# The heads' decay exponents taken in an earlier stage and kept in DRAM, in a one-core hybrid transformer block

## The chip, the cores and the metric

One Trainium2 chip, of which the kernel uses one core. The metric is device time in microseconds (us) of one execution. The kernel before takes 2649.45 us (median of three runs, 2648.09 to 2649.64).

## The reference

One layer of a block over 1024 latent tokens and a context of 256, all of width 1024, in float32. After a first feed-forward part, one input projection gives q, k, v, gates, and five more branches (o, u, vs, ga, gb). Two token mixers run on them and are merged:

```python
dm = b[..., :, None] - b[..., None, :] + lic[..., None, :]
dm = jnp.where(tri, dm, -jnp.inf)
m_t = jnp.maximum(a, jnp.max(dm, axis=-1))
s_ts = jnp.einsum('bhtk,bhsk->bhts', qc, kc) * jnp.exp(dm - m_t[..., None])
...
y_b = spatial_gating(jax.nn.gelu(u), jax.nn.gelu(vs), g_sgu, w_s, b_s)
mixed = jax.nn.sigmoid(ga) * (y_a @ w_a) + jax.nn.sigmoid(gb) * (y_b @ w_b)
return mixed @ w_o
```

The first is an mLSTM with 4 heads of 256, in both directions, scanned in 8 chunks of 128 tokens. Per head, direction and chunk it needs `exp(dm - m_t)`, a 128x128 block that is masked to a triangle; the code calls this P. The second, spatial gating, mixes tokens inside chunks of 128 and multiplies by gelu(u). A second feed-forward part and a norm follow.

## The kernel before

Float32 products run on TensorE as three products of rounded halves: a tile is split by an ACT cast (L145) into its high part and by a DVE subtraction (L146) into the low part. The projections use a seven-product scheme, in which one product is twelve 128x512 matmuls (`pq`, L1377). The weights pass through a queue of steps, `st`: `st.run(n)` runs n of them, and `st.part(n, 3, beside)` or `st.run(n, hook)` calls a function behind each product, so that other work is recorded beside it. Where a step's results leave PSUM, ACT copies them (L1383, L1388, L1391) or DVE adds them to such a copy (L1435), and ACT applies the gate's function (L1434, L1436).

Every engine works in order. All DMAs are issued by SP, in one order, over eight completion semaphores in rotation. A list scheduler places the recorded instructions on their engines; `tc.issue_after(x)` keeps what is recorded under it behind x. PSUM has 4 banks "mm" and 4 banks "sm".

The stages around the change, with their places in the profiled execution:

- 1173 to 1409 us, the sigmoid branches (o, ga, gb): 84 products, with `beside` behind each. It steps two generators, `background2` (further conditioning vectors) and `contexts` (the context's states). `srow`, the rows of decays from which P is built, lie in DRAM before this stage.
- 1418 to 1485 us: the vs branch, written to `vnsp` in DRAM.
- to 1580 us: the u branch. `emit_u` makes gelu(u), and for each pair of column tiles loads the mixing operand `vnp` (L1805, 512 KB) into a ring of buffers. `mix_u` (L1813 to L1819) runs the token mixing `pm` on TensorE, two DVE operations on the result and the store to `ybsp`. Behind the last ten products, `ahead(i)` is called: it starts head 0 (its P, its inter-chunk rows `ib`, its k and q) and loads the mixed rows back from `ybsp` (`yraw`, L1892), split into `yp`.
- 1580 to 1840 us: the w_b product, `pt` (L1856, weights `rawt` L1865), woven with the four heads. Scores `sp` (L1975) are k times q for eight chunks in two halves; `ptk` (L1988) transposes k; both take "sm" banks. DVE multiplies P by `sp` (L1965, `weigh`). The loop takes each chunk in both directions: `pn` (L2009, L2011), a denominator `dn` (ACT L2013, DVE L2014 and L2015), `hm` (L2018), and the state update: ACT makes `wvh` (L1691), TensorE `pu` (L1697), DVE the new `C` (L1698).

Before the change, P of a head is made inside this last stage. `rows` loads `srow`, broadcast to 128 partitions, 128x1024 for each direction (L1937). `coeff` subtracts the column's term with eight ACT operations of 128x128 (L1945) and then takes the minimum with zero and adds the mask with one DVE operation of 128x1024 (L1947). `expo` is one ACT exponential of 128x1024 (L1950). For head 0 that is in `ahead`; for heads 1 to 3 it is in the hook of the loop of the head ahead, at steps 1 to 7. Where the ACT function set changes, an ACT_TABLE_LOAD stands on ACT.

The generator's two masks (`masks[d]`, in the tile `cst`) and the column terms `COL` are loaded or made before the sigmoid stage.

## Time and profile before

| | before |
|---|---|
| median of three runs | 2649.45 us |
| runs | 2648.09, 2649.45, 2649.64 us |
| profiled execution, its own time | 2649.41 us |
| its span, first to last instruction | 2647.6 us |
| granted TensorE clock, mean | 0.998 |
| TensorE (PE) busy | 2632.7 us, 99% |
| VectorE (DVE) busy | 1947.2 us, 74% |
| ScalarE (ACT) busy | 1202.8 us, 45% |

Times inside the kernel are counted from the span's start. "PEld" is the load of weights into TensorE, which overlaps its matmuls. A row of waits gives the engine and line that waited, what it waited for, and us in total, times, longest. In a timeline row, the bracket at the end is the engine's idle time ahead of it and what ended it. "SPq" rows are DMAs being issued, not moved; the time from issue to landing is given apart.

### The profile page before, as it was taken

The numbers are of one execution on the slowest core, as the hardware profiler recorded it, in microseconds if no ns is written. First come the engines' busy times: TensorE is split into PE (matmuls) and PEld (weight loads), VectorE is DVE, ScalarE is ACT, GpSimd is POOL, SyncE is SP. The second block draws the span as 40 slices with busy tenths as digits, with TensorE's granted clock in tenths as the row PEclk, the third lists the DMA queues.
The fourth block names the chain that finished last, engine by engine and source line by source line (L and its number), as shares of the span: only waits on it lengthen the run. The fifth ranks groups of instructions, "written<-read, shape, count | busy, mean of one in ns | idle before, by whom it ended". The sixth has DMA issues, their size and how long they took to land.

```text
span 2647.6 us, 35932 instructions
## 1 busy us (share of the span) xinstructions
PE 2632.7 (99%) x12904; PEld 2213.3 (84%) x12904; DVE 1947.2 (74%) x3490; ACT 1202.8 (45%) x2167; POOL 74.2 (3%) x158
## 2 busy tenths in 40 slices
PE   9999999999999999999999999999999999999998
PEld 6998888888889878888888888888888888888887
DVE  7988688687989646787664878777568766665855
ACT  5664444444347525564443454333256444344433
POOL 0000000000000000000000002221000000000000
PEclk9999999999999999999999999999999999999999
DMA  9833344368587122356552466547341333337654
GB/s 314 308 111 136 119 163 167 112 233 309 172 278 263 65 80 91 104 184 197 188 178 105 151 218 243 175 154 267 131 142 41 127 140 115 120 123 277 200 160 178
DMA packets 201234, 452.73 MB, mean 171 GB/s; under 512 B 20320, under 2 KB 54624, under 8 KB 201056
## 3 DMA queue, kind: packets, MB, share of 16 engines
q1 hardware_dynamic: 200624, 450.05, 49.9%
q8 instruction: 101, 1.65, 0.3%
q14 instruction: 77, 0.63, 0.1%
q10 hardware_dynamic: 432, 0.39, 0.0%
HBM read 329.11 MB, written 121.32 MB: 170 GB/s over the span
## 4 chain that ended last, share of the span: by engine, by line
PE 94%; issue 2%; DMA 2%; DVE 1%; ACT 1%; POOL 0%; SPq 0%; POOLq 0%; DVEq 0%; ACTq 0%
PE qa L411 18%; PE pq L1377 17%; PE po L535 14%; PE qb L411 14%; PE pt L1856 10%; PE pr L1296 5%; PE pa L182 2%; PE pc L1165 2%; PE pb L182 2%; PE pn L2011 2%; PE pu L1697 1%; PE pn L2009 1%; PE pkc L1356 1%; PE pvc L1453 1%; PE sp L1975 1%
## 5 line engine op out<-in xcount | busy, mean ns | idle before, releaser
L146 DVE TENSOR_TENSOR ring<-rawq,ring 128x512 fp32r<-128x512 f32 x408 | 281.0, 690 | 225.5 <-ACT ring L145 224.2
L535 PE MATMUL po<-gring,wring 128*128 128x512 f32 (+1 forms) x1896 | 423.5, 384 | 0.0
L535 PEld LDWEIGHTS po<-gring,wring 128*128 128x128 f32 x1896 | 349.6, 188 | 69.9
L145 ACT CAST ring<-rawq 128x512 fp32r<-128x512 f32 x408 | 253.4, 622 | 312.3 <-PE pq L1377 87.0
L411 PE MATMUL qa<-fc,ring 128*128 128x512 f32 x1056 | 252.4, 389 | 0.0
L411 PEld LDWEIGHTS qa<-fc,ring 128*128 128x128 f32 x1056 | 198.2, 188 | 41.5 <-DVE fc L146 0.4
L1377 PE MATMUL pq<-fc,ring 128*128 128x512 f32 x864 | 208.5, 394 | 0.0
L145 ACT CAST wring<-rw 128x512 fp32r<-128x512 f32 x154 | 95.8, 623 | 217.2 <-PE po L535 183.0
L1377 PEld LDWEIGHTS pq<-fc,ring 128*128 128x128 f32 x864 | 162.2, 189 | 33.4
L1856 PE MATMUL pt<-yp,ring 128*128 128x512 f32 x768 | 184.8, 394 | 0.0
L1856 PEld LDWEIGHTS pt<-yp,ring 128*128 128x128 f32 x768 | 143.1, 188 | 28.2
L146 DVE TENSOR_TENSOR wring<-rw,wring 128x512 fp32r<-128x512 f32 x154 | 105.6, 686 | 81.4 <-ACT wring L145 81.0
L1377 PE MATMUL pq<-fa,ring 128*128 128x512 f32 x576 | 142.4, 395 | 0.0
L1377 PE MATMUL pq<-fb,ring 128*128 128x512 f32 x576 | 138.5, 394 | 0.0
L1377 PEld LDWEIGHTS pq<-fb,ring 128*128 128x128 f32 x576 | 107.7, 188 | 23.8 <-issue 0.2
L411 PE MATMUL qa<-fa,ring 128*128 128x512 f32 x528 | 127.0, 390 | 0.0
L411 PE MATMUL qa<-fb,ring 128*128 128x512 f32 x528 | 126.5, 390 | 0.0
L411 PE MATMUL qb<-fb,ring 128*128 128x512 f32 x528 | 126.5, 389 | 0.0
L411 PE MATMUL qb<-fc,ring 128*128 128x512 f32 x528 | 126.3, 389 | 0.0
L411 PE MATMUL qb<-fa,ring 128*128 128x512 f32 x528 | 126.2, 389 | 0.0
L1377 PEld LDWEIGHTS pq<-fa,ring 128*128 128x128 f32 x576 | 106.9, 188 | 22.3 <-DVE ring L146 0.2
L793 DVE SCALAR_TENSOR_TENSOR adacc<-adapg,sc,adacc 128x512 f32<-128x512 f32 x154 | 111.7, 745 | 15.7 <-DMA adapg<-in_w_ada_dram 14.7
(366 smaller groups left out, 4643.6 us busy)
## 6 DMA issues: line engine op xcount, KB each, us to landing
adapg<-in_w_ada_dram SPq DMA_DIRECT2D x144, 256.0 KB, 3.6
fsp<-fhl SPq DMA_DIRECT2D x66, 512.0 KB, 2.7
gring<-fsp SPq DMA_DIRECT2D x66, 512.0 KB, 4.1
raw<-in_w1i_dram SPq DMA_DIRECT2D x44, 512.0 KB, 5.3
graw<-fsp SPq DMA_DIRECT2D x88, 256.0 KB, 3.6
rawq<-in_w1i_dram SPq DMA_DIRECT2D x38, 512.0 KB, 3.7
rawq<-in_w2i_dram SPq DMA_DIRECT2D x38, 512.0 KB, 3.6
fsp<-p SPq DMA_DIRECT2D x66, 256.0 KB, 2.2
```

What stands on the lines that cost most here:

```text
L145: hi = S.copy(hl[:, 0, :], src)
L146: return hi, V.tensor_sub(hl[:, 1, :], src, hl[:, 0, :].bitcast(F32))
L182: T.matmul(pt, x, y, start=first and i == 0, stop=i == n - 1, skip_group_check=True)
L411: T.matmul(pt, hl[:, x, sl], pages[p][k][:, y, :], start=first and i == 0, stop=i == 11, skip_group_check=not first)
L535: T.matmul(pt[:, cs], w[:, x, sl], g[:, y, cs], start=grp and kp == 0 and i == 0, stop=kp == NFP - 1 and i == 2, skip_group_check=not grp)
L793: eng.scalar_tensor_tensor(acc, pgt, sc2[:, q, k:k + 1], acc, ALU.mult, ALU.add)
L1165: T.matmul(pt, hl[d // 4][:, x, sl], g[:, y, :], start=f == 0 and d % 2 == 0 and i == 0, stop=f == NF - 1 and i == 2, skip_group_check=True)
L1296: T.matmul(self.pt[m], pg[:, x, sl], hl[:, y, :], start=first and k == 0 and i == 0, stop=k == 3 and i == 2, skip_group_check=not first)
L1356: T.matmul(self.cp[:, o:o + 256], hl[:, x, k * 128:(k + 1) * 128], hnc[kc][:, y, :], start=p == 1 and k == 0 and i == 0, stop=p in (2, 4) ...
L1377: T.matmul(pt, hl[:, x, k * 128:(k + 1) * 128], pg[k][:, y, :], start=first and k == 0 and i == 0, stop=k == 3 and i == 2, skip_group_chec ...
L1856: T.matmul(pt, hl[:, x, k * 128:(k + 1) * 128], pg[:, y, :], start=kh + k + i == 0, stop=kh == 1 and k == 3 and i == 2)
L2011: T.matmul(pn[:, 0:257], qi[:, c_, :], self.C[d][:, c_, :], start=False, stop=c_ == 1)
```

## The change

A DRAM tensor `xsp` of 4 MB is added. A third generator, `exponents`, is stepped behind each product of the sigmoid stage. For each head, direction and half it loads 128x512 of `srow` by broadcast, waits three calls, does four ACT operations and one DVE operation on it (what `coeff` did), and two calls later has stored the result to `xsp`. There are 16 such pieces of five calls: 80 of the 84. `Head.rows` now loads P from `xsp` and `coeff` is gone; what is left in the heads' stage is the exponential, recorded at steps 4 and 6. Head 0's exponentials go by halves of 128x512, both directions' first half ahead of the second.

In `ahead`, the loads of head 0's P and most of the `yraw` loads come later: the latter behind the last `vnp` load, P behind the first w_b load. The buffers of two of the `yraw` pairs become tiles of 128x512.

```diff
+    xsp = dr.tile([2, NH, 128, 1024], F32, name="xsp")
...
+    def exponents():
+        for h_ in range(NH):
+            for d in range(2):
+                cb = COL[:, 0, 64 * d:64 * d + 40].rearrange("p (i h) -> p h i", h=4)[:, h_, 2:10]
+                for hf in range(2):
+                    x = fl("xp", "xp", (128, 512), F32, 2)
+                    nc.sync.dma_start(x, srow[d, h_, 0, 4 * hf:4 * hf + 4].rearrange("n t -> (n t)").partition_broadcast(128))
+                    x3 = x.rearrange("p (n t) -> p n t", n=4)
+                    for _ in range(3):
+                        yield
+                    for n in range(4):
+                        S.activation(x3[:, n, :], x3[:, n, :], AF.Identity, bias=cb[:, 4 * hf + n:4 * hf + n + 1], scale=-1.0)
+                    V.scalar_tensor_tensor(x3, x3, 0.0, masks[d].unsqueeze(1).to_broadcast([128, 4, 128]), ALU.min, ALU.add)
+                    yield
+                    nc.sync.dma_start(xsp[d, h_, :, hf * 512:(hf + 1) * 512], x)
+                    yield
...
+        next(bg4, None)
         steps_[0] += 1
...
-            nc.sync.dma_start(vnp[ct], vnsp.rearrange("n p c -> p n c")[:, :, ct * 128:(ct + 1) * 128])
+            ureads["v"] = nc.sync.dma_start(vnp[ct], vnsp.rearrange("n p c -> p n c")[:, :, ct * 128:(ct + 1) * 128])
...
-                nc.sync.dma_start(t, a[name][dt][:, kh * 512:(kh + 1) * 512])
+                asked_b.append(nc.sync.dma_start(t, a[name][dt][:, kh * 512:(kh + 1) * 512]))
...
-                nc.sync.dma_start(pg, srow[d, self.h, 0].rearrange("n t -> (n t)").partition_broadcast(128))
+                nc.sync.dma_start(pg, xsp[d, self.h])
...
-        def coeff(self, d, ns=range(8)):
...
-        def expo(self, d):
-            S.activation(self.pg[d], self.pg[d], AF.Exp)
+        def expo(self, d, sl=slice(0, 1024)):
+            S.activation(self.pg[d][:, sl], self.pg[d][:, sl], AF.Exp)
...
         if i == 0:
-            heads[0].rows()
             heads[0].inter()
-            early.extend(page_raws(ybsp, 0, 0, "yraw", 1))
-            early.extend(page_raws(ybsp, 0, 2, "ring2", 2))
-            early.extend(page_raws(ybsp, 1, 0, "ring2", 2))
-        elif i in (2, 3):
-            heads[0].coeff(i - 2)
+            early.extend(page_raws(ybsp, 0, 0, "yraw"))
+        elif i == 3:
             page_splits(yb, [early.pop(0) for _ in range(2)])
-        elif i == 4:
-            early.extend(page_raws(ybsp, 1, 2, "yraw", 1))
+        elif i == 5:
+            heads[0].kq()
+        elif i == 7:
+            with tc.issue_after(ureads["v"].ins):
+                early.extend(page_raws(ybsp, 0, 2, "ring2"))
+                early.extend(page_raws(ybsp, 1, 0, "ring2"))
+                early.extend(page_raws(ybsp, 1, 2, "yraw"))
             page_splits(yb, [early.pop(0) for _ in range(2)])
-        elif i == 6:
-            heads[0].kq()
-            page_splits(yb, [early.pop(0) for _ in range(2)])
+        elif i == 8:
+            with tc.issue_after(asked_b[0].ins):
+                heads[0].rows()
+            page_splits(yb, [early.pop(0) for _ in range(4)])
...
-        for d in range(2):
-            heads[0].expo(d)
+        for hf in range(2):
+            for d in range(2):
+                heads[0].expo(d, slice(hf * 512, (hf + 1) * 512))
...
-                elif t in (2, 3, 5, 6):
-                    heads[-1].coeff(int(t > 3), range(4) if t in (2, 5) else range(4, 8))
-                elif t in (4, 7):
+                elif t in (4, 6):
                     heads[-1].expo(int(t > 4))
```

Line numbers of the changed kernel differ by 1 up to the added generator, and by 20 or less behind it.

On SP, around the last load of `vnp` at the end of the u branch, before:

```order
L1922 DMA qT<-qsp 128x1024
L1805 DMA vnp<-vnsp 128x8x128
L1922 DMA qT<-qsp 128x1024
L1892 DMA yraw<-ybsp 128x512 x2
L1819 DMA ybsp<-mx 128x512 x2
L1892 DMA yraw<-ybsp 128x512
L1937 DMA P<-srow 128x1024 x2
L1892 DMA yraw<-ybsp 128x512 x3
L1805 DMA vnp<-vnsp 128x8x128
L1819 DMA ybsp<-mx 128x512
L1865 DMA rawt<-in_w_b_dram 128x512
L1892 DMA yraw<-ybsp 128x512 x3
```

The same place on SP after the change (L1944 is the load of qT, L1825 that of vnp, L1839 the store to ybsp, L1914 the yraw load, L1959 the load of P, L1885 the w_b weights):

```order
L1944 DMA qT<-qsp 128x1024
L1825 DMA vnp<-vnsp 128x8x128
L1944 DMA qT<-qsp 128x1024
L1839 DMA ybsp<-mx 128x512
L1825 DMA vnp<-vnsp 128x8x128
L1839 DMA ybsp<-mx 128x512
L1914 DMA yraw<-ybsp 128x512 x6
L1885 DMA rawt<-in_w_b_dram 128x512
L1959 DMA P<-xsp 128x1024
L1839 DMA ybsp<-mx 128x512
L1959 DMA P<-xsp 128x1024
L1885 DMA rawt<-in_w_b_dram 128x512
```

The last vnp load moved ahead of a store, of six yraw loads and of both loads of P.

On PE, from the last products of the u branch into the first heads' work, before:

```order
L1377 MATMUL pq<-fa,ring 128x512 x6
L1377 MATMUL pq<-fc,ring 128x512 x16
L1813 MATMUL pm<-wsr,vnp 128x128 x4
L1377 MATMUL pq<-fc,ring 128x512 x2
L1813 MATMUL pm<-wsr,vnp 128x128 x4
L1377 MATMUL pq<-fc,ring 128x512 x6
L1813 MATMUL pm<-wsr,vnp 128x128 x4
L1975 MATMUL sp<-qT,kT 128x128 x16
L1988 MATMUL ptk<-cst,kT 128x128 x8
L1856 MATMUL pt<-yp,ring 128x512 x12
L1988 MATMUL ptk<-cst,kT 128x128 x4
```

The same place on PE after the change (L1378 is the product, L1833 the mixing, L1989 the scores, L2002 the transposes, L1876 the w_b product):

```order
L1378 MATMUL pq<-fa,ring 128x512 x6
L1378 MATMUL pq<-fc,ring 128x512 x6
L1833 MATMUL pm<-wsr,vnp 128x128 x4
L1378 MATMUL pq<-fc,ring 128x512 x12
L1833 MATMUL pm<-wsr,vnp 128x128 x4
L1378 MATMUL pq<-fc,ring 128x512 x6
L1833 MATMUL pm<-wsr,vnp 128x128 x4
L1989 MATMUL sp<-qT,kT 128x128 x16
L2002 MATMUL ptk<-cst,kT 128x128 x8
L1876 MATMUL pt<-yp,ring 128x512 x5
L2002 MATMUL ptk<-cst,kT 128x128 x4
```

The first mixing matmuls of this piece moved ten products' matmuls earlier, and the third transpose group has five w_b matmuls ahead of it in place of twelve.

On ACT, around head 0's exponentials, before (the casts are L145, the transposes' copies kh L1990):

```order
L145 CAST yp<-yraw 128x512
L1436 ACTIVATE ug<-ug 128x512
L1950 ACT_TABLE_LOAD
L1950 ACTIVATE P<-P 128x1024 x2
L1990 CAST kh<-ptk 128x512 x2
L145 CAST ring<-rawt 128x512
```

The same place on ACT after the change (the gelu is L1437, the casts L146, kh L2004):

```order
L146 CAST yp<-yraw 128x512 x2
L1437 ACTIVATE ug<-ug 128x512
L146 CAST yp<-yraw 128x512
L1964 ACT_TABLE_LOAD
L1964 ACTIVATE P<-P 128x512
L146 CAST yp<-yraw 128x512
L1964 ACTIVATE P<-P 128x512 x3
L2004 CAST kh<-ptk 128x512 x3
```

A cast of yp now stands between the last gelu and the table load, and another between the first and the second half of the exponentials.

More of the change, by code (lines that the diff above doesn't have):

```diff
@@ L1769, in beside @@
             next(bg3, None)
+        next(bg4, None)
         steps_[0] += 1
     st.part(ns, 3, beside)
-    for g_ in (bg2, bg3):
+    for g_ in (bg2, bg3, bg4):
         for _ in g_:
@@ L1886, in _build, with page_raws @@
     tiles("w_b", AHEAD, yb, fin_b, True)
-    def page_raws(src, tb, k, tag, bufs):
-        pg = fl(tag, "yraw", (128, 1024), F32, bufs)
+    def page_raws(src, tb, k, tag):
+        if tag == "ring2":
+            pg = fl(tag, "yraw", (128, 1024), F32, 2)
         res = []
         for i in range(2):
-            r_ = pg[:, i * 512:(i + 1) * 512]
+            r_ = pg[:, i * 512:(i + 1) * 512] if tag == "ring2" else fl(tag, "yraw", (128, 512), F32, 2)
             nc.sync.dma_start(r_, src[tb, k + i])
@@ L1936, in rows @@
                 pg = self.pg[d] = fxpage("P", F32, (128, 1024))
-                nc.sync.dma_start(pg, srow[d, self.h, 0].rearrange("n t -> (n t)").partition_broadcast(128))
+                nc.sync.dma_start(pg, xsp[d, self.h])
                 for hf in range(2):
                     self.P[d, hf] = pg[:, hf * 512:(hf + 1) * 512]
-        def coeff(self, d, ns=range(8)):
-            cb = COL[:, 0, 64 * d:64 * d + 40].rearrange("p (i h) -> p h i", h=4)[:, self.h, 2:10]
-            p3 = self.pg[d].rearrange("p (n t) -> p n t", n=8)
-            for n in ns:
-                S.activation(p3[:, n, :], p3[:, n, :], AF.Identity, bias=cb[:, n:n + 1], scale=-1.0)
-            if 7 in ns:
-                V.scalar_tensor_tensor(p3, p3, 0.0, masks[d].unsqueeze(1).to_broadcast([128, 8, 128]), ALU.min, ALU.add)
-        def expo(self, d):
-            S.activation(self.pg[d], self.pg[d], AF.Exp)
+        def expo(self, d, sl=slice(0, 1024)):
+            S.activation(self.pg[d][:, sl], self.pg[d][:, sl], AF.Exp)
         def inter(self):
@@ L2077, in _build @@
     for tb in range(2):
-        early.extend(page_raws(ybsp, tb, 4, "ring2", 2))
+        early.extend(page_raws(ybsp, tb, 4, "ring2"))
     with tc.issue_after(ureads[True].ins), tc.issue_after(ureads["m"].ins):
```

2 lines of the change are left out of this document (added).

## The prediction, on record before the changed kernel ran

> **What bounds the kernel now.** I read the head of the page first: whose time is the span.
>
> ```profile
> span 2647.6 us, 35932 instructions
> PE 2632.7 (99%) x12904; PEld 2213.3 (84%) x12904; DVE 1947.2 (74%) x3490; ACT 1202.8 (45%) x2167; POOL 74.2 (3%) x158
> ```
>
> PE is busy for all but 14.9 us, and the diff takes no matmul away. So the change can win only idle time of PE, or time in which PE runs at a lower clock. PE's waits, longest first, say where that is:
>
> ```profile
> PE pm L1813 <- DMA vnp<-vnsp: 2.8, 1, 2.8
> PE pu L1697 <- DVE C L1698: 2.2, 2, 1.2
> ```
>
> One wait of 2.8 us is for the last load of the mixing operand `vnp`; two, 2.2 us together, are for the state update `C` in the heads' loops. The windows of the first (behind the length, PE's busy time; the granted clock is third from the end) show that it costs more than its idle time:
>
> ```profile
> 1570.40:1573.20 2.80, 0.05 (x1) 0.00 (x0) 1.69 (x3) 2.80 (x9) 0.00 (x0) 1.00 1.01 359
> 1573.20:1576.00 2.80, 2.74 (x17) 2.68 (x18) 2.80 (x6) 2.41 (x6) 0.00 (x0) 0.77 0.48 143
> 1576.00:1579.00 3.00, 3.00 (x13) 2.52 (x13) 1.80 (x4) 1.22 (x3) 0.10 (x1) 0.65 0.71 250
> ```
>
> PE stands still, and then runs at 0.77 and 0.65 of the clock. The chain of waits prices this (start, us, what):
>
> ```profile
> 1554.11 2.75 PE pq L1377 x12
> ...
> 1564.09 9.04 DMA vnp<-vnsp
> ...
> 1573.26 1.13 PE pm L1813 x8
> 1574.39 0.50 PE pq L1377 x2
> 1574.89 1.71 PE pm L1813 x8
> 1576.60 2.14 PE pq L1377 x6
> 1578.74 0.89 PE pm L1813 x8
> 1579.63 3.57 PE sp L1975 x32
> 1583.20 0.87 PE ptk L1988 x8
> ```
>
> ```profile
> 1573.26 1.13 PE L1813 MATMUL pm<-wsr,vnp 128*128 128x128 f32 x8 [2.82 <-DMA vnp<-vnsp]
> ```
>
> The second fence is the timeline's row, with the gap ahead of it. From 1573.26 to 1578.74 the same rows take 5.48 us; at the clock of the other rows (pm x8 0.89; 12 pq 2.75, so 0.229 each) they are 0.89 + 0.46 + 0.89 + 1.37 = 3.61. So 1.87 us are lost to the clock, and the place costs 2.82 + 1.87 = **4.69 us**.
>
> A rule of the Trainium skill bears on this: page "TensorE: Matmul & The Clock Gate", Part 1: The HAM clock gate, halves the clock after an idle window of about 3.4 us. The trace has the lower clock after 2.82 us already; by the rule the 1.87 would not have been lost here, and the place would hold 2.82.
>
> **The last `vnp` load: the 4.69 goes.** Here are SP's issues, and PE's product, around it:
>
> ```profile
> 1557.77 1.90 SPq L1819 DMA_DIRECT2D ybsp<-mx  x2
> ...
> 1564.09 0.73 SPq L1805 DMA_DIRECT2D vnp<-vnsp  x1
> ...
> 1566.66 3.79 PE L1377 MATMUL pq<-fc,ring 128*128 128x512 f32 x16
> ```
>
> SP issues in order. Before, four `yraw` loads and both P loads stand between the two (the rows left out, and the order above). After, it stands directly behind the first of those `ybsp` stores, and its buffer is free when the pm group ending about 1557.7 has run. So it is issued near 1557.8, 6.3 us earlier. Its landing times:
>
> ```profile
> DMA to landing us min/median/max: 3.8/5.3/9.0
> ```
>
> It lands between 1561.6 and 1566.8. The scheduler also puts its pm ten matmuls earlier, behind 6 of the 16 `fc` matmuls, at 1566.66 + 6 x 0.229 = 1568.0. The longest landing still leaves 1.2 us, so this wait ends: -4.69.
>
> **What is late next: the third `ptk`.** Without the gap, PE reaches its pm chain at 1570.44 and `sp` at 1570.44 + 3.61 + 0.89 = 1574.94. `sp` takes 3.57 and two ptk groups 0.87: 1579.38. Before, twelve `pt` matmuls follow; in the new order only five (5 x 0.229 = 1.15 us), so the third ptk is due at 1580.53. It needs a PSUM bank: here that is the first `sp`'s, free once DVE has multiplied both of head 0's P by it, which needs head 0's exponentials. The rows of before for that chain:
>
> ```profile
> 1580.03 0.62 ACT L145 CAST yp<-yraw 128x512 fp32r<-128x512 f32 x1
> 1580.55 0.62 ACT L1436 ACTIVATE ug<-ug 128x512 f32<-128x512 f32 x1
> 1581.19 1.28 ACT L1950 ACT_TABLE_LOAD   x1
> 1582.49 2.01 ACT L1950 ACTIVATE P<-P 128x1024 f32<-128x1024 f32 x2
> 1584.68 0.68 DVE L1965 TENSOR_TENSOR P<-P,sp 128x512 f32<-128x512 f32 x1
> ```
>
> The `yraw` loads now go out together behind vnp, from about 1559.8; by their median of 5.2 us (row below) the first data is there near 1565. From there DVE has 16 operations of about 0.7 us in a row (6 yp, 5 of the mixing, 3 more mixing or `ug`, 2 ring), 11.2 us; the last `ug` sum ends about 1576.5. ACT follows: gelu 0.63, yp 0.62, table 1.28, half a P 0.55 (half of the 1.06 of a whole one, further down, and a little), yp 0.62, the second half 0.55, DVE's product 0.68: 1581.4. The yp between these waits for `yraw` loads too:
>
> ```profile
> DMA to landing us min/median/max: 3.2/5.2/8.2
> ```
>
> One of them is issued behind a store at about 1573.4. At 5.2 it lands at 1578.6, and yp to product (0.62 + 1.28 + 0.55 + 0.62 + 0.55 + 0.68) end at 1582.9. If DVE is not late, the ug sum ends 0.7 behind its product (1574.7) and there is no wait; at the longest landing it would be 5.4. I take 1582.4, between 1581.4 and 1582.9 and nearer to the yraw case: a new wait of **+1.9** (0 to 3.0 kept). So 4.69 becomes 2.8.
>
> The Trainium skill, page "ScalarE: Activation LUTs", section What ACT_TABLE_LOAD costs, adds a drain of about 1.38 us to a load of 1.283. In the trace the load takes 1.28 and the exponential starts 0.02 after it; by the page the ptk would be 1.38 later and the sum 2647.2.
>
> **The heads' loops.** Both waits of 2.2 come through P:
>
> ```profile
> 1667.33 0.69 ACT L1945 ACTIVATE P<-P,colpg 128x128 f32<-128x128 f32 x2 [2.27 <-DMA P<-srow]
> 1667.94 0.15 ACT L2013 ACTIVATE dn<-pn 128x1 f32<-128x1 f32 x1
> ```
>
> ```profile
> 1738.15 1.21 DVE L1947 SCALAR_TENSOR_TENSOR P<-P,cst 128x1024 f32<-128x1024 f32 x1
> 1739.39 1.06 ACT L1950 ACTIVATE P<-P 128x1024 f32<-128x1024 f32 x1 [1.01 <-DVE P L1947]
> 1739.41 0.47 DVE L1698 SCALAR_TENSOR_TENSOR C<-C,colpg,pu 128x257 f32<-128x257 f32 x1
> 1739.93 0.39 PE L1697 MATMUL pu<-wvh,kh 128*128 128x258 f32 x1 [1.18 <-DVE C L1698]
> ```
>
> Head 3's loop (1738): DVE's 1.21 us for P stands ahead of C; it is removed, and 1.21 exceeds the wait: **-1.18**. Head 2's loop (1667): the coefficients wait for P's load and `dn` stands behind them; the wait on C is the other 0.99 (2.2 less 1.18). The load stays, and I let it land when it does now; then one exponential of 1.06 stands ahead of dn in place of two coefficients (0.69): **+0.4**. Whether a contiguous load of this size lands sooner, these rows bound (issue to landing in that stretch, kT being contiguous):
>
> ```profile
> kT<-ksp SPq DMA_DIRECT2D x2, 512.0 KB, 5.6
> P<-srow SPq DMA_DIRECT2D x2, 512.0 KB, 6.1
> ```
>
> Half a us is less than the exponential holds up, so I keep +0.4; if it lands a us sooner the wait goes (-1.0), and if it lands behind other loads the wait may triple (+2.0). The other 64 coefficients and 8 minima lie beside a busy PE: 0.
>
> **The sigmoid branches' stage: 0 taken.** It gains per piece (16) one load and one store of 256 KB, four ACT operations and one DVE operation of half this size:
>
> ```profile
> L1945 ACT ACTIVATE P<-P,colpg x64: 386/390/411, 1567.2 to 1737.5; 128x128 f32<-128x128 f32 x64
> ```
>
> That is 64 x 0.390 = 25.0 us on ACT and about 16 x 0.61 = 9.8 on DVE, over 250 us. The stage's fullest window for ACT (PE busy, then PEld, DVE and ACT), and the load most like the new one:
>
> ```profile
> 1160.00:1180.00 20.00, 20.00 (x92) 16.55 (x91) 17.75 (x26) 16.08 (x32) 0.00 (x0) 1.00 0.63 212
> ib<-srow SPq DMA_DIRECT2D x16, 256.0 KB, 5.3
> ```
>
> PE has no gap; per 20 us ACT gets 2.0 more and DVE 0.8, and both fit even here. A piece is used three products after its load, 3 x 2.75 = 8.2 us; the same kind of load, ib from the same rows, lands in 5.3. What hides it is that time plus the split's lead of a product; without that cover each piece could cost what a late P cost head 2, 0.99, so 0 to 15.8.
>
> **The sum.** -4.69 + 1.9 - 1.18 + 0.4 + 0 = -3.6, from the profiled execution's 2649.41 (1.8 above its span; the median of the runs shown is 2649.45): **2645.8 us**.
>
> **The rivals.**
> *No new wait, 24%.* DVE keeps pace, the third ptk finds its bank, and head 2's load lands in time: -4.69 - 1.18 - 1.0 = -6.9, **2642.5**. For it: DVE's 0.75 and 0.68 us operations have gaps in the old trace. Against it: five pt instead of twelve.
> *The new wait stands and the clock drops again, 15%.* +1.87 on the forecast: **2647.7**. For it: 0.77 and 0.65 after 2.82; against, head 3's window, whose 1.18 leaves the clock at 1.00:
>
> ```profile
> 1738.00:1744.00 6.00, 4.82 (x27) 4.02 (x26) 5.41 (x17) 3.53 (x8) 2.13 (x4) 1.00 0.13 44
> ```
>
>  By the 3.4 us of the Trainium skill's page on the clock gate, a gap of 1.9 would not lower it; the trace's 2.82 shows that less than 3.4 can, so the rival keeps its chance.
> *It doesn't do what it says, 14%.* vnp lands later than the 10.2 us it now has, because six yraw loads and P crowd it, or a few pieces of the stage show: only head 3's gain and a share of the 4.69 stay. **2648 to 2652**, 2648.2 where nothing but 1.18 is won.
> *Slower, 10%.* In the sigmoid stage the broadcast loads come late, ACT waits at the head of its queue for xp, the gelu and sum that free PSUM banks and the next weights' casts queue behind it, and PE stops. Price 0.99 each; it decides where landings pass 8.2 us (`yraw`, as large and not a broadcast, reached that). Half the pieces: 2645.8 + 7.9 = 2653.7; three quarters **2657.6**; all 2661.6.
>
> **How the numbers follow.** The forecast has 37%; with the four above that is all. About 0.2% (5.3 us) is what a measurement of this kernel can tell from no change, so faster means under 2644.1: the first rival, 24%. Slower means over 2654.8: the last, 10%. The rest, 66%, is the same. The range leaves out the last rival and the far ends of the first and fourth: 2642.3, just under the full removal, to 2651.0, in the fourth.
>
> **What would show it.** Right: no pm wait on vnp and clock 1.00 over 1570 to 1580; a wait of the third ptk near 1580.5 of 1 to 3 us behind weigh; no DVE operation on P ahead of C in head 3; sixteen ACT groups on xp with PE at 20.00 of 20. Wrong: PE rows waiting for ACT or DVE between 1170 and 1410, an ACT wait for xp, a ptk without wait, or a clock under 0.9 behind it.

## The result, and the profile after

The changed kernel takes 2662.10 us (median of six runs), the kernel before beside it 2648.14: a ratio of 1.0053, 95% interval 1.0040 to 1.0066. The forecast was 2645.8 in a range up to 2651.0. The profiled execution took 2661.46 us, 12.05 more than the one of before. The head of its page, and PE's longest waits (total, times, longest):

```profile
span 2659.6 us, 36014 instructions
PE 2637.4 (99%) x12904; PEld 2213.3 (83%) x12904; DVE 1947.8 (73%) x3498; ACT 1202.1 (45%) x2169; POOL 73.0 (3%) x158
```

```profile
PE pq L1378 <- DVE sg L1436: 5.1, 4, 2.3
PE ptk L2002 <- DVE P L1979: 2.3, 1, 2.3
PE pu L1737 <- DVE C L1741: 2.3, 1, 2.3
PE pu L1698 <- DVE C L1699: 1.5, 2, 1.0
...
PE pu L1737 <- ACT ktc L1728: 0.9, 1, 0.9
```

The wait for vnp is gone, and the third ptk waits 2.3 us, as forecast. New are the first, third and last rows: they lie in the sigmoid branches' stage (`sg` is its branches' tile, L1737 the context's state product). The busy time of the engines in 1170 to 1300 us, before and after:

```profile
1170.00:1300.00 130.00, 130.00 (x576) 106.76 (x575) 94.63 (x155) 62.80 (x129) 0.00 (x0) 1.00 0.65 209
```

```profile
1170.00:1300.00 130.00, 121.66 (x516) 97.64 (x515) 94.13 (x157) 74.28 (x182) 0.00 (x0) 0.97 0.78 252
```

PE stands still for 8.3 us, and the clock falls to 0.97 in the mean. To place the whole difference I compare when the same matmul starts in both traces, at five points: the first context state product (1172.58 us before), the last matmul group of the vs branch (1474.39), the first `sp` (1579.46), the first `pn` (1595.75), the last `pn` (1827.38). The delay against before grows or shrinks between them (the last column goes to the end of the span, which is 11.96 longer):

| us | ahead of the stage | sigmoid stage to vs branch | u branch (vnp) | third ptk | heads' loops | behind |
|---|---|---|---|---|---|---|
| forecast | 0 | 0 | -4.69 | +1.9 | -0.8 | 0 |
| measured | +1.70 | **+13.79** | -4.66 | +2.50 | -1.15 | -0.22 |

The 1.70 ahead of the stage come before anything that the change touches (1.1 of it within the first 10 us). The other runs below have 0.1 to 1.6 there, so it is part of what one execution scatters. From here on "the stage's cost" is the third column, worked out in the same way for every run from its one profiled execution. The executions of one kernel scatter: from the fastest to the slowest, 2.6 us in the changed kernel and 7.3 in the widest run below. Two rows that differ by 2 or 3 us are therefore not told apart.

### The profile page after: what moved, and what is told of

It is laid out like the page before. It is cut to its first block, busy times and chain, and to the rows that moved or that the text cites. A ratio compares the mean times of both kernels' runs of the same rounds, so it can differ in the third digit from the quotient of the medians.

```text
span 2659.6 us, 36014 instructions
## 1 busy us (share of the span) xinstructions
PE 2637.4 (99%) x12904; PEld 2213.3 (83%) x12904; DVE 1947.8 (73%) x3498; ACT 1202.1 (45%) x2169; POOL 73.0 (3%) x158
## 3 DMA queue, kind: packets, MB, share of 16 engines
q8 instruction: 101, 1.65, 0.3%
## 4 chain that ended last, share of the span: by engine, by line
PE 88%; DMA 5%; DVE 3%; issue 2%; ACT 1%; SPq 0%; POOL 0%; POOLq 0%; DVEq 0%; ACTq 0%
PE qa L412 18%; PE po L536 13%; PE qb L412 13%; PE pq L1378 13%; PE pt L1876 10%; PE pr L1297 5%; PE pa L183 2%; PE pc L1166 2%; PE pb L183 2%; DMA adapg<-in_w_ada_dram 2%; PE pn L2025 2%; PE pu L1698 1%; PE pn L2023 1%; PE pkc L1357 1%; PE pvc L1454 1%
## 5 line engine op out<-in xcount | busy, mean ns | idle before, releaser
L146 ACT CAST ring<-rawq 128x512 fp32r<-128x512 f32 x408 | 253.3, 621 | 300.4 <-PE qb L412 72.2
L1378 PE MATMUL pq<-fc,ring 128*128 128x512 f32 x864 | 211.3, 397 | 5.1 <-DVE sg L1436 5.1
L1378 PEld LDWEIGHTS pq<-fc,ring 128*128 128x128 f32 x864 | 163.4, 191 | 40.9 <-DVE sg L1436 6.8
L146 ACT CAST wring<-rw 128x512 fp32r<-128x512 f32 x154 | 95.5, 622 | 218.8 <-PE po L536 187.3
L1876 PE MATMUL pt<-yp,ring 128*128 128x512 f32 x768 | 184.9, 394 | 0.0
L1876 PEld LDWEIGHTS pt<-yp,ring 128*128 128x128 f32 x768 | 142.9, 188 | 28.4 <-DVE yp L147 0.2
L1378 PE MATMUL pq<-fa,ring 128*128 128x512 f32 x576 | 142.6, 395 | 0.1
L1378 PE MATMUL pq<-fb,ring 128*128 128x512 f32 x576 | 138.5, 394 | 0.0
L1378 PEld LDWEIGHTS pq<-fb,ring 128*128 128x128 f32 x576 | 107.6, 188 | 23.9 <-issue 0.2
L1378 PEld LDWEIGHTS pq<-fa,ring 128*128 128x128 f32 x576 | 106.8, 188 | 22.7 <-DVE ring L147 0.5
```

The lines of the kernel that those rows point to most:

```text
L146: hi = S.copy(hl[:, 0, :], src)
L1378: T.matmul(pt, hl[:, x, k * 128:(k + 1) * 128], pg[k][:, y, :], start=first and k == 0 and i == 0, stop=k == 3 and i == 2, skip_group_chec ...
L1876: T.matmul(pt, hl[:, x, k * 128:(k + 1) * 128], pg[:, y, :], start=kh + k + i == 0, stop=kh == 1 and k == 3 and i == 2)
```

## The experiments

Each kernel ran beside the kernel before on the same chip. The costs of the parts, from the traces, stand ahead, since all runs are read by them. "ACT for xp" is ACT's longest single wait, in the stage, for a piece's load or for its buffer, counted also where the trace names no end of it ("issue").

| run | median (before beside it) | stage | u branch | third ptk | heads | ACT for xp |
|---|---|---|---|---|---|---|
| the change | 2662.10 (2648.14) | 13.8 | -4.66 | 2.5 | -1.2 | 5.1 |
| no pieces | 2647.43 (2649.07) | 0.5 | -4.65 | 1.7 | -0.3 | none |
| operations only | 2649.09 (2649.16) | 2.3 | -4.63 | 1.7 | -1.6 | 0.4 |
| no load | 2650.87 (2649.07) | 5.0 | -4.63 | 1.3 | -0.1 | 2.7 |
| moves only | 2659.92 (2649.07) | 12.3 | -4.63 | 3.8 | -1.9 | none |
| loads only | 2652.85 (2649.16) | 6.1 | -4.65 | 1.7 | -2.5 | none |
| POOL's queue | 2678.53 (2648.27) | 33.1 | -4.64 | 3.7 | -2.7 | 6.7 |
| unlinked sums | 2662.50 (2648.27) | 15.9 | -4.63 | 1.5 | -2.0 | 5.7 |
| plain rows | 2658.87 (2648.27) | 12.4 | -4.65 | 1.6 | +0.3 | 4.3 |
| unread load | 2659.86 (2649.16) | 10.9 | -4.67 | 1.3 | -1.7 | 3.5 |
| small moves | 2650.45 (2648.90) | 3.0 | -4.63 | 1.9 | -1.0 | 2.0 |
| paced | 2649.12 (2649.07) | 2.6 | -4.64 | 1.2 | -1.6 | none |
| paced, more traffic | 2649.56 (2648.90) | 3.8 | -4.63 | 2.2 | -2.5 | 1.8 |
| spread, late load | 2663.85 (2649.81) | 18.2 | -4.64 | 1.7 | -2.8 | 5.7 |
| order only | 2650.10 (2649.16) | 0.6 | -4.64 | 2.0 | +3.6 | none |
| paced, exponentials first | 2648.53 (2648.27) | 1.3 | -4.65 | 2.0 | -0.4 | none |
| paced, ptk split | 2648.11 (2648.90) | 2.8 | -4.67 | -0.1 | +0.2 | none |

**Which part of a piece costs?** My theory: ACT comes to a piece's operations before its load has landed, and what frees PSUM stands behind them. Rivals: the added operations crowd out others, or the added bytes make other transfers late.

No pieces:

```diff
-        next(bg4, None)
...
-                nc.sync.dma_start(pg, xsp[d, self.h])
+                nc.sync.dma_start(pg, srow[d, self.h, 0].rearrange("n t -> (n t)").partition_broadcast(128))
```

> The changed kernel without its sixteen pieces: the sigmoid branches' stage is as before, P is loaded from the rows by broadcast, and the subtraction, minimum and mask are left out (the exponentials run on scaled raw rows, so P is not the reference's). All theories: the stage's 13.6 us of loss are gone, the 4.7 of the vnp wait stay won, the third ptk still waits about 2.4. 2645 us, 3 below the kernel before. If it stays above 2650, the loss comes from the reordered loads and not from the pieces.

2647.43 us, ratio 0.9995 (0.9986 to 1.0004). The stage is whole (0.5), so the 13.8 are the pieces'. The other terms stay, and add up to -3.3 in its trace; the medians show half of that, within what they can tell.

No load:

```diff
-                    nc.sync.dma_start(x, srow[d, h_, 0, ...].partition_broadcast(128))
...
-                        S.activation(x3[:, n, :], x3[:, n, :], AF.Identity, ...)
+                        S.activation(x3[:, n, :], ident, AF.Identity, ...)
```

> The pieces without their loads: the ACT operations read a resident tile in place of the loaded row, so P is not the reference's; operations, stores and everything else stay. If ACT's wait at the head of its queue for the xp load is the cause, the sigmoid stage loses under 2 us and the time is 2646 to 2648. If the added ACT and DVE operations crowd out what frees PSUM, the stage still loses 10 or more: 2656 to 2661. If DMA traffic is the cause, half of it is left: about 2652.

2650.87, ratio 1.0010 (1.0001 to 1.0018); the stage costs 5.0. Between the first theory's and the traffic's figure. ACT still waits here, up to 2.7 us, for the store that frees a buffer.

Moves only:

```diff
-                    for n in range(4):
-                        S.activation(x3[:, n, :], x3[:, n, :], AF.Identity, ...)
-                    V.scalar_tensor_tensor(x3, x3, 0.0, masks[d]..., ALU.min, ALU.add)
```

> The pieces' loads and stores alone, without their four ACT and one DVE operation (subtraction, minimum and mask left out, exponentials on scaled raw rows). Waiting ACT and crowding both say that the stage is whole again: 2645 to 2647. If the traffic delays the weights and the conditioning rows, the loss stays: 2656 or more.

2659.92, ratio 1.0038 (1.0025 to 1.0051): against my theory. Without any operation of ACT the stage loses 12.3. DVE's waits in its trace show another queue held up, by the conditioning rows `adapg`, which land late:

```profile
DVE adacc L794 <- DMA adapg<-in_w_ada_dram: 26.8, 19, 6.2
```

In the changed kernel that wait is 13.0 in total and at most 1.9, so the two kernels need not lose their time in the same way.

Paced:

```diff
+            sigs[:] = [plus(t, x, pt, AF.Sigmoid)]
...
+                    with tc.issue_after(sigs[0].ins) if sigs else ExitStack():
+                        nc.sync.dma_start(x, srow[d, h_, 0, ...].partition_broadcast(128))
...
+                    with tc.issue_after(sigs[0].ins):
                         for n in range(4):
                             S.activation(x3[:, n, :], x3[:, n, :], AF.Identity, ...)
```

> The whole change, but each piece's load and each piece's ACT and DVE operations are held behind the latest sigmoid recorded at their call, which spreads the sixteen pieces over the stage's 231 us in place of 126, and puts the operations products behind the load. Waiting ACT says that the loss of 13.6 falls under 2 us: 2645 to 2648, below the kernel before. Crowding says that half of it stays, since the work is the same at half the density: about 2652. Traffic says the same as crowding.

2649.12, ratio 1.0002 (0.9993 to 1.0011); the stage costs 2.6. The hold acts on the engine of the instruction named, so only ACT's operations are held; the loads are spread because two buffers are all there is. ACT no longer waits for xp. I took it that the bytes were spread too and that both stories were still open. The window that I showed for the changed kernel says more (DMA share and GB/s at the end of the row):

```profile
1170.00:1300.00 130.00, 129.22 (x569) 105.13 (x568) 99.14 (x163) 71.81 (x164) 0.00 (x0) 1.00 0.79 249
```

The paced kernel moves 249 GB/s there, the changed kernel 252, and PE stands 0.8 us in place of 8.3. What differs is where the operations and the loads stand, not how much is moved.

**Which link leads to PE?**

POOL's queue:

```diff
-                    nc.sync.dma_start(x, srow[d, h_, 0, ...].partition_broadcast(128))
+                    nc.gpsimd.dma_start(x, srow[d, h_, 0, ...].partition_broadcast(128))
...
-                    nc.sync.dma_start(xsp[d, h_, :, hf * 512:(hf + 1) * 512], x)
+                    nc.gpsimd.dma_start(xsp[d, h_, :, hf * 512:(hf + 1) * 512], x)
```

> The changed kernel with the pieces' loads and stores issued by POOL, which has nothing else to do in this stage; the same bytes, the same operations. If the pieces' DMAs, waiting at the head of SP's queue for a landing or an operation, hold up the conditioning rows and weights behind them, the stage's loss falls from 13.8 to under 5: 2650 to 2653. If the bytes themselves slow the other transfers, it stays: 2660 to 2662. If ACT's waits for xp count for themselves, something between is left.

2678.53, ratio 1.0109 (1.0094 to 1.0125). With a queue of their own the stage costs 33.1. On POOL each load stands behind a store that waits for DVE, comes later still, and ACT's longest wait for it is 6.7; the loads also land later there, at a median of 4.7 us against 4.2. The run took one wait away and made another longer, so it does not say what SP's queue costs.

Unlinked sums, for the stage's four vectors:

```diff
-                    ada_acc(V, accs[0], pgt, conds[0], k, k == 0)
+                    ada_acc(V, accs[0]..., ident.unsqueeze(1).to_broadcast([128, 4, 128]), conds[0], k, k == 0)
```

> The changed kernel, in which DVE's sums of the conditioning rows of this stage read a resident tile in place of the rows loaded (the loads are still made), so that DVE never waits for them; the last four modulation vectors are wrong by that. If late conditioning rows at the head of DVE's queue are the link from the pieces' transfers to TensorE, the stage's loss falls from 13.8 to under 5: 2650 to 2653. If the link is ACT's waits for xp or late weights, it stays above 10: 2658 to 2662.

2662.50, ratio 1.0054 (1.0041 to 1.0068); the stage costs 15.9. The waits for conditioning rows are gone (1.6 us are left) and nothing is won, so they are not the link of the changed kernel. ACT's longest wait for a piece is 5.7 here.

Plain rows:

```diff
-                    nc.sync.dma_start(x, srow[d, h_, 0, ...].partition_broadcast(128))
+                    nc.sync.dma_start(x, hsp[hf, 2 * h_ + d])
```

> The changed kernel with each piece's load taken from 128 different rows of another tensor of the same size in DRAM, in place of one row of 2 KB read for all 128 partitions; P is not the reference's. If the loads cost because of their bytes or their place in SP's queue, nothing changes: 2660 to 2662. If reading one row 128 times is slow, or slows others, the loss falls by several us: 2650 to 2656.

2658.87, ratio 1.0036 (1.0022 to 1.0050); the stage costs 12.4. The broadcast is not the main cause; the other 1.4 are within the scatter.

Unread load:

```diff
+                    y = fl("xq", "xq", (128, 448), F32, 1)
+                    nc.sync.dma_start(y, srow[d, h_, 0, ...][0:448].partition_broadcast(128))
...
+                        S.activation(x3[:, n, :], ident, AF.Identity, ...)
```

> The changed kernel, with each piece's load (448 of its 512 columns) landing in a buffer that nothing reads, and ACT's four operations reading a resident tile; operations, stores and nearly all bytes stay, and P is not the reference's. What is taken away is ACT's wait for the load. If that wait, at the head of ACT's queue, is the cause, the sigmoid stage costs what the run without loads cost, about 5: 2650 to 2652. If the loads' bytes or their places in SP's queue are the cause, it still costs 10 or more: 2656 to 2661.

2659.86, ratio 1.0035 (1.0022 to 1.0048); the stage costs 10.9. By its text that speaks for the bytes, but the edit did not do what I said. ACT waits nearly as long in all as in the change, now for the store that frees the buffer, though never longer than 3.5. The execution profiled is the fastest of its five, 4.2 under the median, so the 10.9 is rather too low:

```profile
ACT xp L1774 <- DMA xsp<-xp: 23.8, 11, 3.5
```

So it told nothing apart. Loads only, which is moves only less its stores:

```diff
-                    nc.sync.dma_start(xsp[d, h_, :, hf * 512:(hf + 1) * 512], x)
```

> The pieces' loads alone: no operations, no stores (P from the rows by broadcast, exponentials of scaled raw rows, so P is not the reference's). The loads and stores alone cost the stage 12.3. If that was because a store stands on SP right behind the load that it waits for, and holds SP's queue for it, the loss goes: under 2, about 2647. If the loads' bytes delay the other transfers, at least half stays: 2652 or more.

2652.85, ratio 1.0013 (1.0004 to 1.0022); the stage costs 6.1. About half of the 12.3 of loads and stores goes with the stores; DVE's longest wait for adapg is 5.7. By its text, that is the bytes' side, at its edge.

Operations only, which is the no-load kernel less its stores:

```diff
-                    nc.sync.dma_start(xsp[d, h_, :, hf * 512:(hf + 1) * 512], x)
```

> The pieces' ACT and DVE operations alone, on a resident tile; no loads, no stores (P from the rows by broadcast, without subtraction, minimum and mask). The run without loads cost the stage 5.0. If the added operations crowd those that free PSUM, it still costs 4 to 5: 2649 to 2651. If the stores cost it, the stage is whole: 2645 to 2647.

2649.09, ratio 1.0001 (0.9992 to 1.0011); the stage costs 2.3. This is the price of the work itself.

Order only (the kernel before, with head 0's P and six yraw loads recorded behind the last vnp load):

```diff
+        elif i == 7:
+            with tc.issue_after(ureads["v"].ins):
+                heads[0].rows()
+                early.extend(page_raws(ybsp, 0, 2, "ring2", 2))
...
+            heads[0].coeff(0)
```

> The kernel before with one part alone: head 0's P and six yraw loads behind the last vnp load; the exponents are made in the heads' stage as before. The sigmoid stage costs nothing, the 4.7 of the vnp wait is won, and the third ptk waits longer, since sixteen coefficients (6.2 us of ACT) now stand among the yp casts: 1 to 4. 2646 to 2649. If the vnp wait needed the pieces in DRAM to go, the wait is still there.

2650.10, ratio 1.0004 (0.9995 to 1.0013). The 4.64 are won without any piece in DRAM, and given back in the heads' loops (+3.6), where a wait for C grows to 2.4 and the granted clock is 0.67 behind it, over 1739 to 1744.

**Waits without bytes, bytes without waits.** Small moves:

```diff
-                    nc.sync.dma_start(x, srow[d, h_, 0, ...].partition_broadcast(128))
+                    nc.sync.dma_start(x[:, 0:16], srow[d, h_, 0, 4 * hf]...[0, 0:16].partition_broadcast(128))
...
+                    S.activation(x3[:, 0, 0:16], x3[:, 0, 0:16], AF.Identity, bias=cb[:, 4 * hf:4 * hf + 1], scale=-1.0)
...
-                    nc.sync.dma_start(xsp[d, h_, :, hf * 512:(hf + 1) * 512], x)
+                    nc.sync.dma_start(xsp[d, h_, :, hf * 512:hf * 512 + 16], x[:, 0:16])
```

> The changed kernel with loads and stores of 16 columns in place of 512: one more, short ACT operation reads the 16 loaded columns, so ACT and SP wait for the same chain of landings, and the four operations read a resident tile (P from the rows by broadcast, exponentials scaled; P is not the reference's). Bytes fall from 8.4 MB to 0.3. If the bytes cause the loss, the stage costs what the operations alone cost, about 2: 2647 to 2650. If ACT's waits cause it, most of the 13.8 stays, less what a small landing is shorter: 2653 or more.

2650.45, ratio 1.0007 (0.9998 to 1.0016); the stage costs 3.0. That is the traffic's figure, but ACT's waits had shrunk too, since the small landings are short:

```profile
ACT xp L1772 <- DMA xp<-srow: 7.2, 8, 1.9
ACT xp L1774 <- DMA xsp<-xp: 4.8, 6, 2.0
```

Paced, more traffic (on SP, behind each third product's latest sigmoid store, sixteen in the first half):

```diff
+            with tc.issue_after(puts[0].ins):
+                nc.sync.dma_start(xsq[steps_[0] // 3], hsp[0, steps_[0] % 8])
```

> The paced kernel, in which ACT has no long wait, plus sixteen copies of 256 KB from DRAM to DRAM on SP among the first half of the stage's products: with half the pieces that is at least the changed kernel's traffic there, and the result is the reference's. If the bytes cause the loss, the stage costs 8 to 14 in place of the paced 2.6: 2655 to 2661. If ACT's waits cause it, the stage costs 2 to 5: 2648 to 2651.

2649.56, ratio 1.0005 (0.9996 to 1.0014); the stage costs 3.8. In this kernel's window the last two numbers, DMA share and GB/s, are above those of the changed kernel (0.78 and 252), and PE stands 2.8 us in place of 8.3:

```profile
1170.00:1300.00 130.00, 127.24 (x559) 103.44 (x558) 97.41 (x162) 71.75 (x162) 0.00 (x0) 1.00 0.84 277
```

```profile
ACT xp L1779 <- DMA xp<-srow: 2.3, 2, 1.8
...
DVE adacc L795 <- DMA adapg<-in_w_ada_dram: 24.2, 22, 3.0
```

DVE's waits for adapg are 24.2 in total, and none is over 3.0. More bytes, little loss: the amount of traffic is not the cause. Moves only shifts 256 GB/s in this window, less than here, and loses 12.3, which the amount does not explain.

Spread, late load (the paced kernel, changed in this):

```diff
-                    with tc.issue_after(sigs[0].ins) if sigs else ExitStack():
-                        nc.sync.dma_start(x, srow[d, h_, 0, ...].partition_broadcast(128))
...
                     for _ in range(3):
                         yield
+                    with tc.issue_after(puts[0].ins):
+                        nc.sync.dma_start(x, srow[d, h_, 0, ...].partition_broadcast(128))
                     with tc.issue_after(sigs[0].ins):
```

> The paced kernel, in which each piece's load is issued late, behind the store of the latest sigmoid at the call at which ACT's operations are recorded, so that ACT reaches them before the data is there; the pieces stay spread over the whole stage, and the result is the reference's. If ACT's waits of 3 us and more cost by themselves, the stage costs 8 or more: 2654 or above. If they cost only together with dense transfers, it costs about the paced 2.6: 2648 to 2650.

2663.85, ratio 1.0057 (1.0041 to 1.0074); the stage costs 18.2, with the pieces spread over the whole stage and fewer bytes at a time than the changed kernel (DMA share, GB/s at the end of the row). ACT's waits, and the landing of the stage's loads from `srow` in this kernel:

```profile
1170.00:1300.00 130.00, 126.92 (x552) 103.24 (x550) 95.30 (x158) 66.68 (x151) 0.00 (x0) 0.99 0.74 236
```

```profile
ACT xp L1778 <- DMA xp<-srow: 31.6, 13, 4.9
```

```profile
DMA to landing us min/median/max: 3.5/4.6/5.8
```

The loads land in 4.6 us at the median, against 4.1 in the paced kernel and 4.2 in the change. Half a microsecond of landing does not make waits of 5: they come from where the operation stands behind its load. SP's queue is no other explanation. It stands for the pieces as long in all as in the paced kernel, which loses 2.6 (in the paced kernel L1771 is the load and L1780 the store; in this one L1781 is the store):

```profile
SPq L1771 <- DMA xsp<-xp: 24.6, 11, 5.7
SPq L1780 <- DVE xp L1778: 15.4, 15, 1.9
```

```profile
SPq L1781 <- DVE xp L1779: 19.4, 12, 3.6
SPq L1781 <- DMA xp<-srow: 19.1, 7, 4.2
```

DVE waits less for adapg in all, 14.7 against 19.9, though once for 4.3. So ACT's waits for the pieces cost by themselves. The longest one can be followed to PE. ACT stands for 5.71 us, DVE then for 3.50 behind ACT's cast, and PE for 3.45 behind DVE's sum:

```profile
1347.80 0.40 ACT L1778 ACTIVATE xp<-xp,colpg 128x128 f32<-128x128 f32 x1 [5.71 <-issue]
...
1349.23 0.69 DVE L147 TENSOR_TENSOR ring<-rawq,ring 128x512 fp32r<-128x512 f32 x1 [3.50 <-ACT ring L146]
...
1352.64 0.70 PE L1740 MATMUL pu<-wv,ktc 128*128 128x257 f32 x2 [3.45 <-DVE sg L1436]
```

The trace names no end of that first wait; the load which the operation reads was issued at 1342.02, when the wait began.

**Can the change be made to pay?** Paced, exponentials first (against the paced kernel):

```diff
-    with tc.issue_after(ureads[True].ins), tc.issue_after(ureads["m"].ins):
-        page_splits(yb, early)
     with tc.issue_after(ureads[False].ins):
         for hf in range(2):
             for d in range(2):
-                heads[0].expo(d, slice(hf * 512, (hf + 1) * 512))
+                first = heads[0].expo(d, slice(hf * 512, (hf + 1) * 512))
+    with tc.issue_after(ureads[True].ins), tc.issue_after(ureads["m"].ins), tc.issue_after(first.ins):
+        page_splits(yb, early)
```

> The paced kernel, and head 0's exponentials recorded ahead of the last four splits of yraw, so that no cast of yp stands between the last gelu, the table load and the exponentials on ACT. If the third ptk waits for that chain (2.5 us against the kernel before in the changed kernel, 1.2 in the paced one), the wait falls below 1 us and the time is 2645 to 2648; if it waits for the DVE's backlog, nothing changes: the paced kernel's time.

2648.53, ratio 0.9999 (0.9990 to 1.0008). The third ptk still waits 1.8 us, though no cast stands in the chain any more: PE now has no w_b matmul ahead of it. Paced, ptk split:

```diff
             for hf in range(2):
+                if hf and not weigh:
+                    st.run(1)
                 for n2 in range(2):
                     pt = sm_ps("ptk")
...
     heads[0].scores(False)
-    st.run(2)
+    st.run(1)
```

> The paced kernel with the exponentials first, and one whole w_b product (24 matmuls, 5.5 us) recorded between the second and the third ptk group. The third ptk's wait of 1.2 to 2.5 goes, the stage costs 1 to 2.6, the vnp wait stays won: 2644.5 to 2647, below both kernels. If head 0's first loop then waits for the late kh and kl, the gain is given back there: 2648.

2648.11, ratio 0.9997 (0.9988 to 1.0006). The wait is gone (-0.1), and the trace is 1.5 us shorter than that of before. The medians can't tell it from the kernel before: of 4.67 won, the stage takes 2.8.

## Why the prediction was wrong, point by point

**vnp: right.** Expected: issue near 1557.8, landing within 9.0, the 4.69 gone with the clock's loss. The rows of after, on SP (first) and in the windows:

```profile
1571.97 0.32 SPq L1839 DMA_DIRECT2D ybsp<-mx  x1
1573.26 0.37 SPq L1825 DMA_DIRECT2D vnp<-vnsp  x1
```

```profile
DMA to landing us min/median/max: 3.9/4.6/6.0
```

```profile
1584.00:1588.00 4.00, 4.00 (x26) 3.52 (x25) 4.00 (x7) 1.83 (x4) 0.00 (x0) 1.00 0.68 200
1588.00:1592.00 4.00, 4.00 (x32) 3.75 (x31) 2.91 (x6) 1.24 (x2) 0.11 (x1) 1.00 1.01 358
```

Less the 15.49 us that the kernel is late there, 1573.26 is 1557.77. The term measured 4.66, and 4.6 to 4.7 in all other runs.

**The third ptk: right, somewhat small.** 1.9 forecast, 2.5 measured, with a wait of 2.34. The chain is the one worked out: yp waits for its load, then the table, the halves and DVE's product.

```profile
1592.72 0.62 ACT L146 CAST yp<-yraw 128x512 fp32r<-128x512 f32 x1 [2.03 <-DMA yraw<-ybsp]
...
1594.39 1.28 ACT L1964 ACT_TABLE_LOAD   x1
...
1595.69 0.63 ACT L1964 ACTIVATE P<-P 128x512 f32<-128x512 f32 x1
...
1598.39 0.63 PE L2002 MATMUL ptk<-cst,kT 128*128 128x128 f32 x4 [2.34 <-DVE P L1979]
```

The table load took 1.28 and the exponential started 0.02 us behind it, as in the kernel before; the extra 1.38 of the Trainium skill's page "ScalarE: Activation LUTs", What ACT_TABLE_LOAD costs, are not seen at this place. The second rival, that the clock drops behind this wait, came true in two other runs: in moves only and on POOL's queue the clock fell there, and the term is 3.8 and 3.7.

**The heads' loops: right.** -0.8 forecast, -1.15 measured. Head 3's wait went; head 2's grew less than I thought, to 1.04, since P landed a little sooner. The size is partly luck: followed chunk by chunk, the delay changes by +0.05 at head 2 (+0.4 forecast), by -1.65 at head 3 (-1.18 forecast), and by +0.44 at a wait of 0.42 for C near 1828 that was not forecast. The other runs with the same loops have -2.8 to +0.3. The rows at head 2:

```profile
1680.34 1.06 ACT L1964 ACTIVATE P<-P 128x1024 f32<-128x1024 f32 x1 [1.94 <-DMA P<-xsp]
1681.31 0.15 ACT L2027 ACTIVATE dn<-pn 128x1 f32<-128x1 f32 x1
```

**The sigmoid stage: wrong, 0 forecast, 13.8 measured.** The step that failed is "a piece is used three products after its load, 3 x 2.75 = 8.2 us". That is the distance in which the calls are recorded. The list scheduler placed the operations otherwise, and the built order, which I had, shows it: on SP all sixteen pieces stand ahead of the wgb weights, and three times a load stands right next to the following one. The trace has the sixteen within 1171.5 to 1297.8, 7.9 us each in place of five products' 13.75; behind 1310 the delay grows by another 0.4 only. ACT's operations begin 3.6 to 5.9 us after the load's issue, which leaves no slack over the landing. The density was wrong with it: the sum spread ACT's 25.0 us over 250, 2.0 in 20; they came within 126, 4.0 in 20. Around two pieces, in order of time:

```profile
1279.95 0.41 ACT L1773 ACTIVATE xp<-xp,colpg 128x128 f32<-128x128 f32 x1 [2.85 <-DMA xp<-srow]
...
1281.79 0.69 DVE L1774 SCALAR_TENSOR_TENSOR xp<-xp,cst 128x512 f32<-128x512 f32 x1 [3.96 <-ACT xp L1773]
...
1287.22 0.32 SPq L1768 DMA_DIRECT2D xp<-srow  x1
...
1287.97 1.13 PE L1737 MATMUL pu<-wv,ktc 128*128 128x257 f32 x4 [2.26 <-DVE C L1741]
...
1291.32 0.40 ACT L1773 ACTIVATE xp<-xp,colpg 128x128 f32<-128x128 f32 x1 [5.13 <-DMA xp<-srow]
1291.62 0.60 ACT L146 CAST ring<-rawq 128x512 fp32r<-128x512 f32 x1
...
1292.26 0.69 DVE L147 TENSOR_TENSOR ring<-rawq,ring 128x512 fp32r<-128x512 f32 x1 [2.56 <-ACT ring L146]
...
1295.26 0.96 PE L1378 MATMUL pq<-fc,ring 128*128 128x512 f32 x3 [0.41 <-DVE sg L1436]
```

At the first piece ACT waits 2.85 us, DVE's operation on the piece stands 3.96 for ACT, what is queued on DVE behind it runs late, `C` among it, and PE stands for 2.26. At the second, ACT had reached the operation at 1286.2, a microsecond ahead of the load's issue. It stands for 5.13 us; the cast of the next weights is behind it, DVE's half of the split behind that, the sum `sg` behind that, and PE last, but for 0.41 only: this longest wait of all hardly reaches PE. ACT's waits for xp in the stage (the second row's have no end named):

```profile
ACT xp L1773 <- DMA xp<-srow: 20.3, 9, 5.1
...
ACT xp L1773 <- issue: 5.7, 3, 2.4
```

**The rival was near, for a wrong reason.** "Slower, 10%" named ACT waiting for xp ahead of gelu, sums and casts, and its end for all pieces, 2661.6, is where the kernel landed. But it set the point at landings over 8.2 us. They were 5.9 at most; the operations' place decided. That 16 times 0.99 comes near the 13.8 is luck: PE stands six times, between 0.41 and 2.26 us.

**What one wait costs stays open.** Of the kernels in the table that have the pieces' operations, those in which ACT's longest wait for a piece is up to 2.7 us lose 1.3 to 5.0 in the stage (the operations alone 2.3); 3.5 and more go with 10.9 to 33.1. The sum of the waits parts them in the same way, 12.0 us and less against 21.8 and more, so these runs do not tell the longest wait from the sum. The 2.75 us of the product that PE works on while ACT stands look like a cover, but do not fit: in unread load the waits exceed 2.75 by 1.2 in all, and the stage costs 10.9. Nor does each gap of PE have a long wait of ACT ahead of it. Before the gap of 2.00 near 1269, ACT's last waits at pieces are 1.85, 1.11 and 1.42, and DVE has been working almost without a break since 1256. DVE's wait for adapg is no better measure: 24.2 us in pieces up to 3.0 go with 3.8, 26.8 in pieces up to 6.2 with 12.3 (moves only), but pieces up to 3.7 with 2.3 (operations only). So "PE has no gap" in the old windows told that no wait reached PE, not how much more the queues of ACT and DVE could bear.

**The size** of the 13.8 can be placed. PE has six gaps in the window, 8.3 us together. The clock falls behind two of them, of 2.26 and 2.00; there the delay against before grows by 4.12 and 3.89, 3.7 more than the gaps. One of the two stretches of 24 matmuls, and the following 24 at full clock:

```profile
1269.09 7.35 PE L1378 MATMUL pq<-fc,ring 128*128 128x512 f32 x24 [2.00 <-DVE sg L1436]
1276.28 5.76 PE L1378 MATMUL pq<-fb,ring 128*128 128x512 f32 x24
```

Each of the other four gaps delays PE by 0.3 more than its idle time, 1.2 in all, and 0.5 come behind 1300. What stays open is how the 13.8 divide between ACT's waits and the dense loads and stores. Spread, late load shows that the waits are enough without dense transfers; moves only shows that loads and stores at these places cost 12.3 without any wait of ACT. By which way they do is not shown; the wait for adapg there is a reading of one trace, and was not tried.

## What to carry to other kernels

Where a scheduler places instructions, the distance between a load and its use is what the built order says, not the number of calls between the lines that record them; count the work that stands between them on the engine that will wait. A loop without gaps does not show how much lateness it can still hide: here short, spread waits of ACT cost up to 5.0 us, and longer ones 10.9 and more, though the longest single wait hardly reached PE. The amount of traffic told nothing: with 249 and 252 GB/s PE stood 0.8 and 8.3 us. An experiment that removes a wait has to be read for the wait that replaces it before it counts.

## What the runs showed of the hardware

The clock fell behind gaps shorter than the 2.82 us of before, and not always. In the changed kernel, a gap of 2.26 us was followed by 0.50 and one of 2.00 by 0.65 (first two rows), while the ptk's of 2.34 (third row) and another of 2.26 (last row) were followed by 1.00:

```profile
1202.00:1205.00 3.00, 3.00 (x7) 2.40 (x8) 3.00 (x6) 2.60 (x7) 0.00 (x0) 0.50 0.76 239
...
1269.00:1272.50 3.50, 3.41 (x10) 2.72 (x11) 3.36 (x7) 1.69 (x4) 0.00 (x0) 0.65 0.70 207
...
1598.30:1601.00 2.70, 2.61 (x16) 2.29 (x17) 2.64 (x5) 2.70 (x7) 1.25 (x6) 1.00 0.84 244
...
1288.00:1291.00 3.00, 3.00 (x13) 2.50 (x14) 1.70 (x4) 0.00 (x0) 0.00 (x0) 1.00 0.76 207
```

The 3.4 us of the Trainium skill's page "TensorE: Matmul & The Clock Gate", Part 1: The HAM clock gate, is not a bound below which a gap is free. Both times that the clock fell in this kernel's stage, PE lost 1.9 us more than the gap, as it had before (1.87); a gap without a fall cost 0.3 more than its length. A fall can last longer: in moves only, behind a gap of 4.27, the clock stood at 0.50 over this window:

```profile
1268.30:1275.00 6.70, 5.44 (x13) 4.28 (x14) 3.16 (x6) 1.62 (x3) 0.00 (x0) 0.50 0.91 287
```
